# Two stacked two-layer blocks on one core: a planner with a margin on its durations, convolution taps later in its order, and gates between the head pairs of the last core

## The chip, the core and the metric

The kernel runs on one core of one Trainium2 chip. The time is device microseconds of one execution, taken over several executions; the profile is one more execution with the hardware profiler on. The engines are PE (TensorE, matmuls), DVE (VectorE), ACT (ScalarE), POOL (GpSimd) and SP (SyncE, which issues the transfers).

## What is computed

Two blocks stand one behind the other, each of two layers, for 512 tokens of width 1024 (S = 512, D = 1024), all in float32. The second block takes the output of the first.

```python
# block 1, each of 2 layers
p = rmsnorm(x) @ w_in
c_q, c_kv = rmsnorm(p[:, :384]), rmsnorm(p[:, 384:640])     # latents of q and of k, v
y_attn = mla_attention(c_q @ w_uq, c_kv @ w_ukv, rope(p[:, 640:672]))   # 8 heads
u = a * sigmoid(gt)                                         # a, gt: rest of p, 512 wide each
u = silu(layernorm(dwconv(u, 31 taps) + b))
x = x + concat(y_attn, u) @ w_o
z = dwconv(rmsnorm(x) @ w_up, 3 taps)
x = x + (silu(zg) * zv) @ w_down
# block 2, layer 0: state space mixer; layer 1: HGRN2 mixer (8 heads, chunks of 64)
z, xbc, dt = split(x @ w_in)
y = ssd(silu(conv4(xbc)), softplus(dt))       # 4 groups of 8 heads, chunks of 128
y = group_rmsnorm(y * silu(z)) @ w_out        # the "gate" is silu(z)
x = layer_norm(alpha * x + y)
x = layer_norm(alpha * x + relu(x @ w1)**2 @ w2 + gated per-layer input (PLE))
```

## The kernel before

**Tiling.** Activations lie transposed, 128 features by 512 tokens a tile. Each float32 operand is split into a rounded part and the rest (`hi`, `lo`; a copy and a subtraction), and a product is three matmuls (`mm3`: hi hi, hi lo, lo hi). A dense unit of 128 output features from 1024 inputs is `dense`: 8 x 3 = 24 matmuls of 128x512 into one PSUM bank. Sums over features go through `tok_sum`: squares on ACT, adds of [128 x 512] tiles on DVE or POOL (the last of them inside `tok_sum`), then matmuls against a column of ones (psum 128x1) or transposes; `rstd` makes 1/root on [128 x 4] tiles (DVE, then a power on POOL), and `spread` puts that back onto 128x512 by transposes of a small tile on PE.

**The order.** Nothing is issued while the model is written down. A `Recorder` records 19079 operations in the order in which the Python code calls for them; `schedule` then plans them in a list: of all operations that are ready it takes the one with the earliest start, then with the least priority number `bias - 0.015 * tail + i`, where `i` is the number in the record and `tail` the longest way to the end. `R.bias` is added to what is recorded under it: with 100, an operation stands as if it were recorded 100 operations later. The plan reckons each operation's duration by a formula (`cost`, from sizes and engine), waits between engines by a table (`LAT`), a transfer by its bytes, and an ACT table load at 1283 ns. Operations marked `either` or `other` may go to DVE or POOL, and `copy` to ACT or DVE: the plan picks. It plans POOL's work and DVE's work with two SBUF inputs not to overlap (`shares`). `SLOTS` says how many buffers of a class there are (8 PSUM banks), and `KEEP` how many of them an operation must leave free while older recorded ones still want one: 4 banks of PSUM. The resulting order on each engine, with each choice of engine, is the program; engines run their own queue in order and wait on semaphores. All instructions are issued by one line, L597, so the profile is read by tiles and by place.

**What the change touches.** `Recorder.__init__` (L330) and `cost` (L341); `KEEP` (L616); `conv_tile` (L976) in the first block's mixer, which is called behind each of the 4 head pairs of the attention: 17 taps as `SCALAR_TENSOR_TENSOR psum<-u,V,psum` on DVE into a PSUM bank and 14 taps as ACT products with POOL or DVE adds, the side; behind it come `project("w_o")` for the attention half, the convolution's layer norm (`center`, `tok_sum`, `spread`), silu, and the convolution half of `w_o`. In the state space mixer `core(g, ...)` (L1211) does one group: transposes and state products, then 4 head pairs, each with two broadcast matmuls (psum<-s,n), decays on DVE and ACT, and 64x128 products. `gate(g, ys)` (L1280) does 4 dense units with `Silu` and a product, then the group norm. The loop at the end (L1297 to L1303) records inputs and cores group by group, the last core alone (`ys[3] = core(3, *held)`), and then the 4 gates with the output projections between them. SP's queue holds the weight loads (3 buffers of class `r`).

Of the kernel before, what the change touches and what calls it, by code (L numbers as in the profile page):

```python
# [17 lines left out]
P = 128  # L18
# [301 lines left out]
class Recorder:  # L320
# [9 lines left out]
    def __init__(self):  # L330
        self.ops, self.bias, self.label, self.switch = [], 0, "", 150
        self.greed, self.order_w, self.second, self.eager, self.drag = 0.015, 1.0, 0, 0, 0.5

    def tile(self, cls, shape, dt=F32):
# [6 lines left out]

    def cost(self, eng, meth, args, kw):
        out = kw.get("out", args[0] if args else None)
        n = out.n if isinstance(out, Ap) else 1
# [270 lines left out]
SLOTS = {"psum": 8, "r": 3, "s": 86, "u": 4, "t": 12, "n": 24, "V": 1, "C": 1}  # L615
KEEP = {"psum": 4, "s": 18, "u": 2, "t": 6, "n": 16}  # L616
SIDE_TAPS = 14
# [6 lines left out]
def record(R, xT, pos, wts, vecs, consts, pT, outT, dbg=None, stop=None):  # L624
# [6 lines left out]
    def bank():  # L631
        return R.tile("psum", (P, S), F32)
# [248 lines left out]
    def mixer1(l):  # L881
# [94 lines left out]
        def conv_tile(j):  # L976
            R.label = f"conv{l}"
            acc = bank()
# [7 lines left out]
            for k in range(CONV_K - SIDE_TAPS, CONV_K):  # L986
# [4 lines left out]
                else:  # L991
                    R.either.tensor_add(side, side, t)
            R.vector.tensor_add(conv[j], acc, side)

        att = [pair() for _ in range(4)]
# [132 lines left out]
    def ssd(op):  # L1128
# [81 lines left out]

        def core(g, B, Cm, xs):  # L1211
            R.label = "ssd_core"
# [36 lines left out]
            ys = []  # L1249
            for hp in range(4):  # L1250
                py, pz = bank(), bank()
                ec = tl((P, 3 * P))
# [25 lines left out]
            return ys  # L1278

        def gate(g, ys):  # L1280
            R.label = "ssd_gate"
            for j in range(4):
                ps = bank()
                dense(ps, weights("ssd_w_in_2"), 0, P, op)
                t = tl()
                R.scalar.activation(t, ps, AF.Silu)
                R.other.tensor_mul(ys[j], ys[j], t)
            r = spread(rstd(sumsq(ys), 512, EPS2))
            out = []
            for j in range(4):  # L1290
                R.vector.scalar_tensor_tensor(ys[j], ys[j], vec("nw", g * 4 + j), r, op0=ALU.mult, op1=ALU.mult)
                hi, lo = pair()
                split_from(ys[j], hi, lo, R.either)
                out.append((hi, lo))
            return out

        ys, yo = {}, {}  # L1297
        for g in range(GROUPS):
# [3 lines left out]
            held = t  # L1302
        ys[3] = core(3, *held)  # L1303
        for g in range(GROUPS):
# [351 lines left out]
```

## Time and profile before

| | us |
|---|---|
| median of 3 executions | 2747.29 (2746.51 to 2747.91) |
| profiled execution | 2746.72 |
| its span | 2744.9 |
| PE busy in the span | 2680.1 |
| DVE, ACT, POOL busy | 1878.6, 1176.4, 775.2 |

The span runs from the first to the last instruction; 1.8 us of the profiled execution lie around it. PE is busy for 98% of the span, so what the order of the program can give back is the rest, and the stretches in which PE's clock is granted at half. The views used below give busy time of each engine by stretch of the span, with the mean granted clock (1.00 is full), and the single instructions of PE and DVE around the waits, with the idle time before each and the tile for which it waited.

The stages lie in the span as follows (us): first mixer 28 to 219 (attention from about 100), its feed forward to 680, second mixer 680 to 802, its feed forward to 1195, time steps of the state space mixer 1200 to 1222, its inputs and cores to 1430 (the last core, g = 3, from 1376), gates and output to 1600, layer norm to 1640, MLP to 1960, layer norm 1960 to 1990, HGRN2 mixer to 2270, layer norm to 2350, MLP to 2680, last layer norm and output to the end.

### The profile page before, as it was taken

Reading aid. Unit: us, or ns where it says so; the run is one execution under the profiler, and the core shown is the slowest. Engines: PE = TensorE matmul, PEld = TensorE weight load, DVE = VectorE, ACT = ScalarE, POOL = GpSimd, SP = SyncE. Lnnn points to the kernel's source line nnn. Section 1 sums busy time; section 2 is a strip of 40 time slices with the busy share of each in tenths; the row PEclk is TensorE's granted clock in tenths of the full one; section 3 lists DMA queues with packets and bytes.
Section 4 is the critical chain, followed back from the end, with each engine's and each line's share of the span. In section 5 each row is a group of like instructions: output and inputs, shape, how many; then the busy total and the mean of one; then the engine's idle time right before and its main releaser. Section 6 shows DMA issues by size and latency. Waiting matters only on the chain.

```text
span 2744.9 us, 38876 instructions
## 1 busy us (share of the span) xinstructions
PE 2680.1 (98%) x15054; PEld 2213.4 (81%) x15054; DVE 1878.6 (68%) x3319; ACT 1176.4 (43%) x2151; POOL 775.2 (28%) x645
## 2 busy tenths in 40 slices
PE   9899999999899999999989999999999999999998
PEld 7668888888678888888768898888888889888888
DVE  8997676666977766675885675445677887554546
ACT  4874323345764332343653432222356664322223
POOL 1771010134840111242331421222412123112232
PEclk9999999999999999999999999999999999999999
DMA  5031233231131223331112413223131113232320
GB/s 171 18 108 69 76 103 107 99 111 30 56 108 54 93 92 108 99 103 47 40 62 73 163 55 103 91 101 109 62 108 48 60 66 114 88 108 83 115 93 32
DMA packets 69448, 234.98 MB, mean 86 GB/s; under 512 B 7824, under 2 KB 11152, under 8 KB 69264
## 3 DMA queue, kind: packets, MB, share of 16 engines
q1 hardware_dynamic: 69264, 232.51, 25.3%
q8 instruction: 118, 1.93, 0.3%
q14 instruction: 66, 0.54, 0.1%
HBM read 230.38 MB, written 2.10 MB: 85 GB/s over the span
## 4 chain that ended last, share of the span: by engine, by line
PE 80%; DVE 15%; issue 3%; ACT 2%; POOL 0%; DMA 0%; POOLq 0%; DVEq 0%; ACTq 0%; SPq 0%
PE psum L597 80%; DVE s L597 10%; DVE psum L597 3%; ACT s L597 1%; DVE n L597 1%; ACT L597 0%; DMA r<-wts 0%; POOL n L597 0%; POOL s L597 0%; DVE u L597 0%; DVE t L597 0%; POOL u L597 0%; ACT t L597 0%; POOLq L597 0%; DVEq L597 0%
## 5 line engine op out<-in xcount | busy, mean ns | idle before, releaser
L597 PE MATMUL psum<-s,s 128*128 128x512 f32 (+3 forms) x12944 | 2604.2, 365 | 35.8 <-DVE s L597 16.0
L597 PEld LDWEIGHTS psum<-s,s 128*128 128x128 f32 (+1 forms) x12944 | 2117.8, 185 | 472.8 <-issue 27.3
L597 POOL TENSOR_TENSOR s<-r,s 128x512 fp32r<-128x512 f32 (+1 forms) x342 | 469.4, 1389 | 1062.2 <-ACT s L597 798.7
L597 ACT CAST s<-r 128x512 fp32r<-128x512 f32 (+1 forms) x721 | 407.9, 611 | 402.3 <-DMA r<-wts 390.4
L597 DVE TENSOR_TENSOR s<-s,s 128x256 f32<-128x256 f32 (+5 forms) x625 | 405.8, 672 | 76.7 <-ACT s L597 66.1
L597 DVE TENSOR_TENSOR s<-s,psum 128x512 f32<-128x512 f32 (+2 forms) x400 | 224.0, 591 | 297.6 <-PE psum L597 297.2
L597 POOL TENSOR_TENSOR s<-s,s 128x512 f32<-128x512 f32 (+4 forms) x215 | 257.1, 1206 | 514.2 <-DVE s L597 348.3
L597 DVE TENSOR_TENSOR s<-r,s 128x512 fp32r<-128x512 f32 (+1 forms) x527 | 378.2, 746 | 5.9 <-ACT s L597 3.4
L597 ACT ACTIVATE s<-s 128x512 f32<-128x512 f32 (+1 forms) x338 | 186.5, 579 | 211.8 <-DVE s L597 210.6
L597 ACT ACTIVATE s<-u,V 128x512 f32<-128x512 f32 x200 | 142.5, 763 | 264.8 <-DVE u L597 264.6
L597 ACT ACTIVATE s<-psum 128x512 f32<-128x512 f32 (+2 forms) x174 | 91.7, 528 | 373.6 <-PE psum L597 370.3
L597 DVE SCALAR_TENSOR_TENSOR s<-u,V,s 128x512 f32<-128x512 f32 x176 | 143.1, 814 | 50.0 <-ACT s L597 46.8
L597 DVE SCALAR_TENSOR_TENSOR s<-psum,s 128x512 f32<-128x512 f32 (+1 forms) x88 | 55.3, 639 | 113.4 <-ACT s L597 109.4
L597 DVE TENSOR_TENSOR u<-psum,s 128x512 f32<-128x512 f32 x88 | 60.6, 689 | 83.0 <-PE psum L597 82.8
L597 POOL TENSOR_TENSOR n<-n,n 128x4 f32<-128x4 f32 (+1 forms) x32 | 35.0, 1095 | 282.1 <-DVE n L597 281.6
L597 ACT COPY s<-psum 128x512 f32<-128x512 f32 (+4 forms) x137 | 69.6, 531 | 86.2 <-PE psum L597 85.2
L597 ACT CAST s<-s 128x512 fp32r<-128x512 f32 (+2 forms) x125 | 72.7, 592 | 75.4 <-DVE s L597 74.7
L597 DVE CAST s<-r 128x512 fp32r<-128x512 f32 (+1 forms) x148 | 62.7, 434 | 54.5 <-DMA r<-wts 54.3
L597 ACT ACT_TABLE_LOAD x68 | 87.2, 1283 | 21.2 <-DVE s L597 19.3
L597 PE MATMUL psum<-C,s 128*128 128x128 f32 (+1 forms) x532 | 80.3, 271 | 12.7 <-ACT s L597 6.0
L597 DVE SCALAR_TENSOR_TENSOR psum<-u,V,psum 128x512 f32<-128x512 f32 x128 | 91.3, 743 | 0.3
L597 PEld LDWEIGHTS psum<-C,s 128*128 128x128 f32 x532 | 63.6, 146 | 30.7 <-ACT s L597 12.8
(87 smaller groups left out, 875.3 us busy)
## 6 DMA issues: line engine op xcount, KB each, us to landing
r<-wts SPq DMA_DIRECT2D x415, 512.0 KB, 3.6
r<-wts SPq DMA_DIRECT2D x12, 256.0 KB, 2.8
r<-wts SPq DMA_DIRECT2D x8, 384.0 KB, 3.1
s<-xT SPq DMA_DIRECT2D x8, 256.0 KB, 6.1
s<-pT SPq DMA_DIRECT2D x8, 256.0 KB, 4.0
outT<-s SPq DMA_DIRECT2D x16, 128.0 KB, 1.8
r<-wts SPq DMA_DIRECT2D x9, 128.0 KB, 2.0
V<-vecs SPq DMA_DIRECT2D x1, 480.5 KB, 6.6
```

Of the source, the lines that this page charges most:

```text
L597: getattr(eng, meth)(*[res(a) for a in args], **{k: res(v) for k, v in kw.items()})
```

## The change

Four edits, and the new function `gate_unit`:

1. `self.margin = 1.12`: the plan reckons every operation but transfers as 12% longer. The waits between engines, the transfers and the table load keep their numbers.
2. `KEEP["psum"]` from 4 to 2.
3. `conv_tile` is recorded with `R.bias = 100`, so its taps, side and sum stand later in the order.
4. The dense unit of a gate becomes `gate_unit`. The 4 units of group 0 are recorded in front of the 4 head pairs of the last core; `gate(0)` then does the rest.

```diff
+        self.margin = 1.12
     def cost(self, eng, meth, args, kw):
+        return self.duration(eng, meth, args, kw) * (1.0 if eng == "sync" else self.margin)
+
+    @staticmethod
+    def duration(eng, meth, args, kw):
...
-KEEP = {"psum": 4, "s": 18, "u": 2, "t": 6, "n": 16}
+KEEP = {"psum": 2, "s": 18, "u": 2, "t": 6, "n": 16}
...
         def conv_tile(j):
-            R.label = f"conv{l}"
+            R.label, R.bias = f"conv{l}", 100
...
             R.vector.tensor_add(conv[j], acc, side)
+            R.bias = 0
...
-        def core(g, B, Cm, xs):
+        def core(g, B, Cm, xs, between=None):
...
             for hp in range(4):
+                if between:
+                    between(hp)
+                    R.label = "ssd_core"
                 py, pz = bank(), bank()
...
+        def gate_unit(ys, j):
+            R.label = "ssd_gate"
+            ps = bank()
+            dense(ps, weights("ssd_w_in_2"), 0, P, op)
+            t = tl()
+            R.scalar.activation(t, ps, AF.Silu)
+            R.other.tensor_mul(ys[j], ys[j], t)
+
         def gate(g, ys):
             R.label = "ssd_gate"
-            for j in range(4):
-                ps = bank()
-                dense(ps, weights("ssd_w_in_2"), 0, P, op)
-                t = tl()
-                R.scalar.activation(t, ps, AF.Silu)
-                R.other.tensor_mul(ys[j], ys[j], t)
+            for j in range(0 if g else 4, 4):
+                gate_unit(ys, j)
...
-        ys[3] = core(3, *held)
+        ys[3] = core(3, *held, lambda j: gate_unit(ys[0], j))
```

The record holds the same 19079 operations and the same matmuls. The order and the choices of engine come out anew over the whole program: DVE has 3006 instructions where it had 3110, POOL 694 for 637, ACT 2101 for 2048 (a few table loads among them), and SP the same 482. In the HGRN2 cores 16 operations go from DVE to POOL; in the two MLPs 35 do. Three places follow; a name is class, slot and number of a tile, `V` the vectors, `C` the constants, and the number of a tile is not the same in the two kernels. All instructions of the changed kernel are issued at L603.

**Place 1: the norms of the q and the kv latents in the first mixer (93 to 96 us).** DVE before: three `n5` rows are the norm of q, `psum2` and `psum4` rows are taps of the convolution, and `s81_885` is the last add for the sum of kv, for which PE waits.

```order
L597 TENSOR_SCALAR n5_905<-psum7_887 128x4
L597 SCALAR_TENSOR_TENSOR s66_908<-psum6_749,V0_65,s76_890 128x512
L597 TENSOR_TENSOR n5_905<-n5_905,n3_525 128x4
L597 SCALAR_TENSOR_TENSOR psum2_620<-u2_71,V0_65,psum2_620 128x512
L597 SCALAR_TENSOR_TENSOR psum4_691<-u0_67,V0_65,psum4_691 128x512
L597 TENSOR_SCALAR n5_905<-n5_905 128x4
L597 TENSOR_TENSOR s81_885<-s81_885,s85_922 128x512
L597 SCALAR_TENSOR_TENSOR s58_942<-psum0_793,V0_65,s67_927 128x512
```

DVE in the changed kernel, the same three rows of q's norm (here `n5_881`):

```order
L603 TENSOR_SCALAR n5_881<-psum7_856 128x4
L603 TENSOR_SCALAR s79_418<-s79_418,V0_65 128x512
L603 TENSOR_TENSOR n5_881<-n5_881,n3_687 128x4
L603 TENSOR_TENSOR s83_891<-r0_553,s70_804 128x512
L603 TENSOR_SCALAR n5_881<-n5_881 128x4
L603 SCALAR_TENSOR_TENSOR s77_901<-s46_786,V0_65,s79_418 128x512
L603 SCALAR_TENSOR_TENSOR s85_912<-psum0_765,V0_65,s74_899 128x512
L603 SCALAR_TENSOR_TENSOR psum1_602<-u2_71,V0_65,psum1_602 128x512
```

The add for kv (`s76_858`) stands on POOL there, behind the power of q's norm (`n6_910`):

```order
L603 TENSOR_TENSOR s57_651<-s57_651,s2_657 128x512
L603 TENSOR_TENSOR s44_583<-s44_583,s56_664 128x512
L603 TENSOR_TENSOR n6_910<-n5_881,n0_74 128x4
L603 TENSOR_TENSOR s76_858<-s76_858,s52_894 128x512
L603 TENSOR_TENSOR s57_651<-s57_651,s59_670 128x512
L603 TENSOR_TENSOR s44_583<-s44_583,s61_676 128x512
```

The last of q's three rows stood at place 152 of DVE's list and stands at 136; the taps between the three rows are gone, and the add for kv has left DVE.

**Place 2: the last core of the state space mixer (1402.7 to 1412 us).** PE before: `s35_9122,n3_2103` rows are broadcasts of a head pair, 128x128 and 64x128 rows its products.

```order
L597 MATMUL psum3_12360<-s35_9122,n3_2103 128x512
L597 MATMUL psum2_12364<-s24_12354,s29_12284 128x512
L597 MATMUL psum0_12348<-s51_11983,s18_12337 128x128
L597 MATMUL psum6_12357<-s51_11983,s18_12337 128x128
L597 MATMUL psum4_12376<-s35_9122,n3_2103 128x512
L597 MATMUL psum7_12389<-s51_11983,s83_12326 128x128
L597 MATMUL psum7_12389<-s51_11983,s18_12337 128x128
L597 MATMUL psum5_12398<-s35_9122,n3_2103 128x512
L597 MATMUL psum1_12403<-s35_9122,n3_2103 128x512
L597 MATMUL psum0_12348<-s51_11983,s17_12370 128x128
L597 MATMUL psum6_12357<-s51_11983,s17_12370 128x128
L597 MATMUL psum3_12415<-s74_12386,s38_12291 64x128
```

PE in the changed kernel around the same broadcasts (`s79_10132,n6_2355`); `psum7_12345`, `psum6_12296` and `psum3_12413` are dense units of group 0's gate:

```order
L603 MATMUL psum2_12385<-s79_10132,n6_2355 128x512
L603 MATMUL psum7_12345<-s66_10533,s50_11973 128x512
L603 MATMUL psum6_12296<-s83_10530,s15_11987 128x512
L603 MATMUL psum7_12345<-s1_10507,s37_11995 128x512
L603 MATMUL psum6_12296<-s25_10555,s60_11971 128x512
L603 MATMUL psum0_12395<-s79_10132,n6_2355 128x512
L603 MATMUL psum7_12345<-s42_10514,s26_11992 128x512
L603 MATMUL psum6_12296<-s23_10570,s60_11971 128x512
L603 MATMUL psum7_12345<-s47_10543,s26_11992 128x512
L603 MATMUL psum6_12296<-s25_10555,s15_11987 128x512
L603 MATMUL psum7_12345<-s42_10514,s38_12016 128x512
L603 MATMUL psum3_12413<-s67_10477,s56_11997 128x512
```

From the last input row to the last row of the core stood 100 core and 42 gate rows, the gate rows behind the first 98 of the core; now 100 core and 111 gate rows, and gate rows stand between core rows from the 65th core row on.

**Place 3: the layer norm behind the first MLP (1968.9 us).** PE before: the `C0_156,n16` row spreads mean and deviation, 128x512 rows with `s14_16850` belong to PLE's projection, and 128x256 rows with `s25_16658` (and `s23_16748`) need the normalized tiles.

```order
L597 MATMUL psum4_17162<-s69_16739,s14_16850 128x512
L597 MATMUL psum7_17165<-C0_156,n16_17152 128x128 x2
L597 MATMUL psum5_17168<-s69_16739,s14_16850 128x512
L597 MATMUL psum6_17173<-s69_16739,s14_16850 128x512
L597 MATMUL psum3_17186<-s80_17177,s25_16658 128x256
L597 MATMUL psum3_17186<-s81_17205,s25_16658 128x256
```

PE in the changed kernel from the spread on; the 128x256 rows that need the normalized tiles have `s67_16658`:

```order
L603 MATMUL psum6_17175<-C0_152,n16_17166 128x128 x2
L603 MATMUL psum5_17160<-s72_16754,s54_16854 128x512
L603 MATMUL psum7_17162<-s27_17157,s25_16842 128x512
L603 MATMUL psum7_17162<-s42_16750,s31_16868 128x512
L603 MATMUL psum7_17162<-s72_16754,s54_16854 128x512
L603 MATMUL psum2_17164<-s27_17157,s25_16842 128x512
L603 MATMUL psum2_17164<-s42_16750,s31_16868 128x512
L603 MATMUL psum2_17164<-s72_16754,s54_16854 128x512
L603 MATMUL psum0_17196<-s29_17185,s67_16658 128x256
L603 MATMUL psum3_17169<-s27_17157,s25_16842 128x512
L603 MATMUL psum3_17169<-s42_16750,s31_16868 128x512
L603 MATMUL psum3_17169<-s72_16754,s54_16854 128x512
```

Behind the spread stood two 128x512 rows and then a row that needs the norm; now seven stand there, then one such row, and three more 128x512 rows before the second (which stands two rows behind the last one shown). The layer norm at the end of the second MLP has the same pattern in both kernels.

## Rows read from the trace of the kernel before

**Rows 1.** Page: busy us (share) x instructions; chain of waits by engine

```profile
PE 2680.1 (98%) x15054; PEld 2213.4 (81%) x15054; DVE 1878.6 (68%) x3319; ACT 1176.4 (43%) x2151; POOL 775.2 (28%) x645
...
PE 80%; DVE 15%; issue 3%; ACT 2%; POOL 0%; DMA 0%; POOLq 0%; DVEq 0%; ACTq 0%; SPq 0%
```

**Rows 2.** Busy in a stretch of the second MLP, 128x512 matmuls alone

```profile
2400.00:2500.00 100.00, 100.00 (x436) 81.61 (x435) 50.33 (x72) 24.90 (x45) 19.73 (x16) 1.00 0.30 100
```

**Rows 3.** Waits of PE: tile <- tile waited for, total us, times, longest

```profile
PE psum L597 <- DVE s L597: 24.9, 30, 3.3
PE psum L597 <- ACT s L597: 15.6, 23, 1.7
PE psum L597 <- issue: 6.5, 3, 2.5
```

**Rows 4.** Busy by stretch: length, PE, weight loads, DVE, ACT, POOL, clock, DMA

```profile
28.00:110.00 82.00, 75.86 (x332) 60.87 (x331) 79.47 (x138) 56.45 (x94) 41.78 (x30) 0.96 0.19 60
110.00:200.00 90.00, 82.33 (x465) 57.83 (x464) 88.98 (x134) 69.03 (x150) 63.15 (x55) 1.00 0.23 77
...
680.00:790.00 110.00, 99.31 (x553) 73.42 (x552) 103.50 (x162) 84.11 (x176) 79.94 (x67) 1.00 0.22 69
...
1200.00:1222.00 22.00, 17.95 (x142) 16.51 (x141) 17.51 (x40) 10.58 (x26) 14.97 (x14) 1.00 0.18 55
...
1376.00:1430.00 54.00, 46.92 (x306) 34.29 (x305) 50.34 (x121) 31.20 (x52) 25.01 (x21) 0.97 0.08 29
...
1960.00:1990.00 30.00, 26.89 (x192) 25.51 (x192) 26.49 (x73) 15.33 (x38) 14.86 (x17) 0.89 0.11 36
...
2055.00:2270.00 215.00, 206.95 (x2770) 176.96 (x2770) 167.83 (x415) 149.23 (x288) 39.49 (x34) 0.99 0.18 60
2270.00:2350.00 80.00, 76.08 (x597) 73.30 (x596) 62.05 (x136) 31.11 (x73) 28.01 (x27) 1.00 0.28 94
...
2680.00:2700.00 20.00, 16.85 (x119) 15.62 (x118) 19.29 (x53) 8.19 (x19) 9.08 (x11) 0.91 0.01 2
```

**Rows 5.** Timeline of PE, 47 to 102: start, us, operation, [idle before <- releaser]

```profile
50.55 1.11 PE L597 MATMUL psum<-C,n 128*128 128x128 f32 x4 [2.53 <-POOL n L597]
...
96.52 1.05 PE L597 MATMUL psum<-C,s 128*128 128x1 f32 x8 [3.35 <-DVE s L597]
```

**Rows 6.** Timeline of PE, 692 to 700 us, the second mixer

```profile
696.99 1.09 PE L597 MATMUL psum<-C,n 128*128 128x128 f32 x8 [3.32 <-DVE n L597]
```

**Rows 7.** Timeline of PE, 1967.5 to 1979 us, behind the spread

```profile
1970.50 0.38 PE L597 MATMUL psum<-s,s 128*128 128x256 f32 x1 [0.70 <-ACT s L597]
1973.18 1.01 PE L597 MATMUL psum<-s,s 128*128 128x256 f32 x3 [2.30 <-DVE s L597]
```

**Rows 8.** Timeline of PE, 2684 to 2692 us, the last layer norm

```profile
2687.72 0.62 PE L597 MATMUL psum<-s,s 128*128 128x256 f32 x3 [2.30 <-DVE s L597]
```

**Rows 9.** Timeline of PE, 112 to 130 us, the attention

```profile
121.02 0.50 PE L597 MATMUL psum<-s,s 128*128 128x512 f32 x1 [1.03 <-DVE s L597]
```

**Rows 10.** Timeline of PE, 1395 to 1430 us, the last core

```profile
1405.36 0.50 PE L597 MATMUL psum<-s,n 128*128 128x512 f32 x1 [0.64 <-DVE s L597]
...
1411.32 5.41 PE L597 MATMUL psum<-s,s 128*128 128x128 f32 x44 [1.06 <-DVE s L597]
```

**Rows 11.** Page, groups: operation xcount | busy us, mean ns | idle before

```profile
L597 POOL TENSOR_TENSOR s<-s,s 128x512 f32<-128x512 f32 (+4 forms) x215 | 257.1, 1206 | 514.2 <-DVE s L597 348.3
L597 DVE TENSOR_TENSOR s<-r,s 128x512 fp32r<-128x512 f32 (+1 forms) x527 | 378.2, 746 | 5.9 <-ACT s L597 3.4
...
L597 DVE SCALAR_TENSOR_TENSOR psum<-u,V,psum 128x512 f32<-128x512 f32 x128 | 91.3, 743 | 0.3
```

**Rows 12.** Timeline of PE, 195 to 222 us, centre of the convolution's norm

```profile
199.60 1.12 PE L597 MATMUL psum<-s,t 128*128 128x512 f32 x2
```

**Rows 13.** Timeline of DVE, 197 to 222 us, its first split

```profile
215.11 0.42 DVE L597 CAST s<-s 128x512 fp32r<-128x512 f32 x1
```

**Rows 14.** Timeline of DVE, 100 to 118 us, beside POOL

```profile
108.05 1.72 DVE L597 TENSOR_TENSOR s<-r,s 128x512 fp32r<-128x512 f32 x1
```

## The prediction

> **What bounds the kernel now.** The page comes first. PE is busy 98% of the span and has 80% of the chain of waits, DVE 15% [rows 1]. So the kernel is bound by PE's work, which this change leaves as it is. What an order can win is the span less PE's busy time, 2744.9 - 2680.1 = 64.8 us, and what a lower clock costs. In a dense stretch 436 matmuls of 128x512 took 100.00 us, PE busy for all of it [rows 2]: 0.229 us each, the price of a PE row that covers a wait. PE's waits are put down mostly to DVE's tiles (24.9 us in 30 waits) and ACT's (15.6 us in 23) [rows 3].
>
> Next, the table by stretch, for where that time lies [rows 4]. The reader is to see that idle stands in few stretches, and a lower granted clock beside it. For each I add the idle time and (1 - clock) x length, which is what is lost while the clock stands at 1.2 in place of 2.4 GHz:
>
> - 28 to 110: 82.00 - 75.86 = 6.1 idle, 0.04 x 82 = 3.3 clock: 9.4
> - 110 to 200: 7.7, clock full
> - 680 to 790: 10.7, clock full
> - 1200 to 1222: 4.1, clock full
> - 1376 to 1430: 7.1 + 0.03 x 54 = 8.7
> - 1960 to 1990: 3.1 + 0.11 x 30 = 6.4
> - 2055 to 2270: 8.1 + 0.01 x 215 = 10.2
> - 2270 to 2350: 3.9, clock full
> - 2680 to 2700: 3.2 + 0.09 x 20 = 5.0
>
> Together 66 us, the most that this change can work on. In the first three stretches and the last core DVE is busy for 79.47 of 82, 88.98 of 90, 103.50 of 110 and 50.34 of 54 us: there DVE is the bound, and what matters is how much of its work stands ahead of each row for which PE waits. Behind the layer norms it is how many PE rows cover DVE's chain.
>
> Last, the waits themselves. The longest are 2.53 us at 50.55 (the first norm) and 3.35 at 96.52 (the sum of kv) [rows 5], 3.32 at 696.99 [rows 6], 0.70 and 2.30 behind the spread at 1970 [rows 7], and 2.30 at 2687.72 [rows 8]. Shorter ones stand in the attention, as 1.03 at 121.02 [rows 9], and in the last core [rows 10].
>
> **The change part by part.** Operations and matmuls are the same, so no edit has a cost of its own; each moves rows. The margin does it everywhere, by making operations look long against the waits and transfers that keep their numbers; the bias and the gates do it in two places.
>
> *28 to 110.* In front of DVE's first norm row stand 8 rows fewer (place 72 for 80), and PE has 12 rows to do before the spread for 10. The norm came 2.53 us late [rows 5]; I leave 0.7 of it: 1.8 won. The add for kv stood behind the last row of q's norm, at place 152 of DVE; that row now has place 136. Sixteen rows at 0.58 us (DVE's mean here, 79.47 / 138 [rows 4]) are 9 us, so PE's sum for q sets the time then, and not DVE's queue. The add itself is on POOL, behind the power of q's norm, and takes 1.2 us there [rows 11]; PE has 10 rows more (2.3 us) to do before it needs the result. The wait of 3.35 closes but for 0.3: 3.0 won. Each of these waits was followed by half clock; of those 3.3 us I take 2.3. Sum 7.
>
> *110 to 200.* The bias lets the taps be passed. The splits of the first head pair's Q and K stood at places 182 to 190 of DVE and stand at 154 to 168; the last attention row has place 296 for 310, the last tap 287 for 284. DVE's rows up to the convolution's norm become fewer by some 14, or 8 to 10 us. DVE is 98% busy from 28 to 200, so both stretches can win what DVE loses, about 10, and the 3 us that DVE is idle: 13 at most. I take 4 here, 11 for both. What is late next is the chain of the convolution's norm: from the centre's matmul at 199.60 [rows 12] to the first split at 215.53 [rows 13] it took 15.9 us. From that matmul to the first row of `w_o`'s convolution half PE had 99 rows (22.7 us) and has 74 (places 765 to 839): 16.9 us. That covers it by 1 us, and I cost it at nothing, with -1 as a bound; without that cover it is the slower rival below.
>
> *680 to 790.* The same in the second layer. The wait of 3.32 [rows 6] shrinks by 2.8, since the norm's rows come earlier; the splits stand at place 805 for 830, the last attention row at 938 for 963, the last tap at 929 for 902. DVE's 6.5 us of idle leave more room, and the convolution's cover stays 94 rows. I take 7 of 10.7.
>
> *1200 to 1222.* The norm's spread stands 3 PE rows later, and three `lo` tiles stand one behind another on POOL. Bounds 0 and -1.6; I take -1.
>
> *1376 to 1430.* The first 64 rows of the core, to about 1390, have no gate row between them, as before, so they keep their waits. Behind them four waits, from 0.64 at 1405.36 to 1.06 at 1411.32 [rows 10], are 2.8 us, and the clock's fall 1.6; 0.6 more stands in front of them. Up to the last core row stand 111 gate rows for 42: 69 x 0.229 = 16 us of cover for these 5.0. The rows come from a stretch behind that stays dense. With them 4 `Silu`, 4 products and some table loads come into the core's queues; POOL (25.01 of 54 us busy) and ACT (31.20) have room [rows 4]. I take 4.
>
> *1960 to 1990 and 2680 to 2700.* Behind the spread stood two 128x512 rows and then a row of the norm; now 7 and 3 more, eight more in all, 1.8 us of cover for 0.70 and 2.30 [rows 7], and DVE has two products fewer in front of the second tile (0.4 us each). The rows taken from ahead of the spread covered nothing that waited. I leave 1 us of idle; the half clock behind it (3.3, and 1.8) then mostly goes: 5 and 3.5 won.
>
> *2055 to 2270.* Sixteen operations of the HGRN2 cores go to POOL. DVE and ACT have 167.83 and 149.23 us of work in 215 [rows 4], so there is slack; the three `issue` waits (6.5 us [rows 3]) are not waits for another engine's tile, and stay. Bounds -6 and 3; I take 0. *2270 to 2350:* 16 more MLP rows stand before the first row that waited: 2 won of 3.9. The dense stages stay.
>
> *New waits.* A list planned anew waits where none did. The nearest rows are PE's waits for ACT, 15.6 us in 23 [rows 3], 0.7 each: I take 4 of them, -3, with 0 and -12 as bounds.
>
> Sum: 7 + 4 + 7 - 1 + 4 + 5 + 3.5 + 0 + 2 - 3 = 28.5. From the profiled execution, 2746.7, that is 2718.2; the median stands 0.6 above it. I say 2718. With half of what is won (32.5 / 2 = 16) and new waits at their bound, 4 us are left: 2743. With all that the terms name (13 + 10.7 + 5 + 6.4 + 5 + 3.9 = 44) and 3 in the HGRN2 mixer: 2700.
>
> **The rivals.** *The load comes back through POOL.* DVE has 104 rows fewer, POOL 57 more. A DVE subtraction beside POOL took 1.72 us at 108.05 [rows 14], where its group's mean is 0.746 [rows 11]: 1 us more. As a mechanism here: eight more POOL rows in the first two mixers each cost DVE 1 us where it is the bound, 8 lost, and DVE no longer runs ahead, so that the mixers win half, 9 less: 2718 + 17 = 2735. Against it, taps read one tile from SBUF, and the plan keeps POOL and such DVE work apart. The Trainium skill, "SBUF — State Buffer", section "SBUF: two separate sides", states that a DVE instruction with two SBUF inputs and a POOL one that reads SBUF lock each other out for a whole instruction; the row at 108.05 agrees with that.
>
> *The plan does not do what it says.* The plan of before foresaw no such waits either. If a longer reckoning only shifts them to other tiles, the mixers win nothing, and the layer norms (8.5) and the core (4) stand against new waits at their bound, 12: no change, 2747. For it speaks that 53 waits on DVE and ACT [rows 3] are spread over a whole program that is planned anew.
>
> *Slower: the taps come too late.* The norm of the convolution cannot start before the last tap. Between the last attention row and the centre's matmul PE has 11 rows (2.5 us), and the cover behind it 1 us: 3.5 us, or 5 taps of 0.743 us [rows 11], can end behind the attention at no cost; each further tap costs its 0.743 us in each layer. It outweighs the 28.5 us when each layer loses 14.3, from (14.3 + 3.5) / 0.743 = 24 taps; at 40 of the 68 it is 2 x (29.7 - 3.5) = 52 lost: 2770. Against it, the attention's last row stands behind the last tap on DVE in both layers.
>
> **How the numbers follow.** The forecast has 0.62, with its own range from 2700 to 2743; the load on POOL 0.15 (2735); waits only shifted 0.12 (2747, to either side); taps too late 0.08 (2770); 0.03 for more than the listed gains. The range from 2698 to 2744 leaves out the slower rival, most of the third case and the tail below, 2 in 10. A measurement tells about 0.2%, 5.5 us, from no change: faster is below 2741.8. Faster: 0.61 + 0.15 + 0.03 = 0.79; within 0.2%: 0.10 of the shifted waits and 0.01 of the forecast, 0.11; slower: 0.08 + 0.02 = 0.10.
>
> **What would show it.** In the table by stretch of the changed kernel: idle of 2 us in place of 6.1 between 28 and 110 with the clock above 0.98; DVE still over 95% busy in the attention, with about 4 us of idle in each mixer; no wait above 0.5 us in the core's second half; the clock at 0.97 or more behind the two spreads; dense stages still full. It would be wrong if the mixers' idle stayed near 18 us with DVE's subtractions well above 0.75 us (POOL), if waits of over 1 us stood where PE had none (shifted), or if PE waited for the convolution's centre behind the attention (slower).

## The result

The changed kernel takes 2716.45 us (median of 4 executions, 2715.73 to 2719.6); the kernel before took 2746.9 beside it. The ratio is 0.9893, 95% interval 0.9876 to 0.9910: 29 us less by the ratio, 1.1%, where 2718 us had been forecast. Over all runs and chips the kernel before took 2743.84 to 2754.78 us, so what follows compares ratios, each to the kernel before on the same chip.

The page of the changed kernel, with busy time, share and count of each engine and the chain of waits by engine [rows 1]:

```profile
PE 2666.4 (98%) x15054; PEld 2214.5 (82%) x15054; DVE 1859.3 (69%) x3215; ACT 1214.9 (45%) x2206; POOL 831.4 (31%) x702
...
PE 94%; DVE 4%; ACT 1%; issue 1%; DMA 0%; POOL 0%; SPq 0%; ACTq 0%; POOLq 0%; DVEq 0%
```

DVE's part of the chain fell from 15% to 4%. PE's idle is 2714.0 - 2666.4 = 47.6 us, for 64.8; PE's busy time fell by 13.7 us with the same matmuls. Half clock hides in it: 18 matmuls of 128x512 took 4.29 us at 98.36 and 5.84 at 107.46, behind a long wait, and the granted clock from 107 to 110 was 0.54 (both are shown below). PE's waits (tile, tile waited for, total, times, longest) are as many us on DVE as before and half as many on ACT [rows 3]:

```profile
PE psum L603 <- DVE s L603: 24.4, 21, 4.8
PE psum L603 <- ACT s L603: 7.8, 11, 1.6
PE psum L603 <- issue: 7.6, 5, 3.3
```

A longest wait on DVE of 4.8 us is new. Since all stages shift in time, I matched every PE instruction of the two traces to its recorded operation and compared when the last one of a stage ends. The shares, in us won in the profiled executions (spans 2744.9 and 2714.0), beside what was forecast:

| stage | forecast | won |
|---|---|---|
| start, first mixer to the last row of its inputs | 7 | 10.0 |
| first attention, `w_o`, feed forward | 4 | -1.9 |
| second mixer and feed forward | 7 | 13.2 |
| time steps, inputs of the state space mixer | -1 | 1.9 |
| last core and gates | 4 | 6.9 |
| output, layer norm, first MLP | 0 | -1.3 |
| layer norm behind the first MLP | 5 | 0.5 |
| HGRN2 mixer | 0 | 2.8 |
| its layer norm, second MLP | 2 | -0.2 |
| last layer norm and end | 3.5 | -1.0 |
| new waits, anywhere | -3 | (in the rows above) |
| sum | 28.5 | 30.9 |

The sum came out 2.4 us from the forecast, and several of its rows miss by 3 to 6 us, to both sides: that they cancel is luck. The stretches in which PE waited before, in the changed kernel (length, PE, weight loads, DVE, ACT, POOL, clock, DMA share [rows 4]):

```profile
28.00:107.00 79.00, 74.66 (x343) 61.10 (x341) 73.94 (x125) 57.42 (x94) 37.50 (x29) 1.00 0.19 59
107.00:110.00 3.00, 2.54 (x6) 2.11 (x7) 2.64 (x5) 0.00 (x0) 0.03 (x1) 0.54 0.00 0
110.00:200.00 90.00, 84.30 (x475) 61.52 (x475) 85.22 (x130) 63.19 (x139) 61.13 (x56) 0.98 0.13 43
680.00:771.00 91.00, 89.54 (x512) 66.24 (x511) 87.10 (x138) 72.75 (x155) 64.04 (x57) 1.00 0.14 43
1353.00:1374.00 21.00, 16.01 (x120) 11.55 (x118) 20.00 (x50) 16.53 (x28) 12.35 (x11) 0.99 0.07 25
1374.00:1417.00 43.00, 43.00 (x253) 34.11 (x254) 33.15 (x70) 25.99 (x39) 13.95 (x13) 0.96 0.12 38
```

The second mixer is nearly full now (1.5 us idle in 91). The core's second half, from 1374, is full, and its first half keeps its waits. Between 28 and 107 the waits for the first norm and for the sum of kv are gone and the clock is full; all 4.3 us of idle there are one new wait, which ends at 107.46. PE, then DVE, then POOL around it (start, length, operation, idle before):

```profile
98.36 4.29 PE L603 MATMUL psum<-s,s 128*128 128x512 f32 x18
107.46 5.84 PE L603 MATMUL psum<-s,s 128*128 128x512 f32 x18 [4.81 <-DVE s L603]
```

```profile
101.30 1.40 DVE L603 SCALAR_TENSOR_TENSOR psum<-u,V,psum 128x512 f32<-128x512 f32 x2
102.61 5.04 DVE L603 CAST s<-s 128x512 fp32r<-128x512 f32 x2
107.57 2.12 DVE L603 TENSOR_TENSOR s<-s,s 128x512 fp32r<-128x512 f32 x3
```

```profile
95.83 11.20 POOL L603 TENSOR_TENSOR s<-s,s 128x512 fp32r<-128x512 f32 x9 [0.99 <-DVE s L603]
114.96 0.13 POOL L603 MEMSET u<- 128x1 f32 x2 [7.93 <-DVE psum L603]
```

Two casts that take 0.42 us each took 5.04 together (the first 4.71 of them), and came free when POOL's nine adds and subtractions, 1.25 us each and without a pause, ended at 107.03. PE waits for the first cast, the `hi` part of the first head pair's Q.

The plan had foreseen this clash. The section on the order names only DVE's work with two SBUF inputs, but `shares` keeps copies from SBUF to SBUF apart from POOL's work as well. In the plan's own times POOL pauses from 103.1 to 105.9 us, and DVE's two casts and the subtractions behind them fall into that pause. In the program there is only the order of each queue: POOL had nothing to wait for and went on.

### The profile page after: what moved, and what is told of

It reads as the page before. It is cut to its first block, busy times and chain, and to the rows that moved or that the text cites. A ratio compares the mean times of both kernels' runs of the same rounds, so it can differ in the third digit from the quotient of the medians.

```text
span 2714.0 us, 38873 instructions
## 1 busy us (share of the span) xinstructions
PE 2666.4 (98%) x15054; PEld 2214.5 (82%) x15054; DVE 1859.3 (69%) x3215; ACT 1214.9 (45%) x2206; POOL 831.4 (31%) x702
## 4 chain that ended last, share of the span: by engine, by line
PE 94%; DVE 4%; ACT 1%; issue 1%; DMA 0%; POOL 0%; SPq 0%; ACTq 0%; POOLq 0%; DVEq 0%
PE psum L603 94%; DVE s L603 3%; ACT s L603 1%; DVE psum L603 0%; POOL s L603 0%; DVE n L603 0%; DMA s<-xT 0%; DMA r<-wts 0%; ACT L603 0%; SPq L603 0%; POOL n L603 0%; ACTq L603 0%; POOLq L603 0%; DVEq L603 0%
## 5 line engine op out<-in xcount | busy, mean ns | idle before, releaser
L603 PE MATMUL psum<-s,s 128*128 128x512 f32 (+5 forms) x12944 | 2601.0, 365 | 34.7 <-DVE s L603 22.8
L603 PEld LDWEIGHTS psum<-s,s 128*128 128x128 f32 (+2 forms) x12944 | 2118.8, 185 | 459.0 <-issue 35.3
L603 POOL TENSOR_TENSOR s<-r,s 128x512 fp32r<-128x512 f32 (+1 forms) x371 | 509.2, 1386 | 1122.6 <-ACT s L603 869.3
L603 ACT CAST s<-r 128x512 fp32r<-128x512 f32 (+1 forms) x738 | 420.4, 613 | 380.0 <-DMA r<-wts 369.2
L603 DVE TENSOR_TENSOR s<-s,s 128x512 fp32r<-128x512 f32 (+4 forms) x605 | 398.8, 681 | 75.0 <-ACT s L603 66.1
L603 DVE TENSOR_TENSOR s<-s,psum 128x512 f32<-128x512 f32 (+2 forms) x400 | 225.5, 592 | 280.7 <-PE psum L603 278.6
L603 POOL TENSOR_TENSOR s<-s,s 128x512 f32<-128x512 f32 (+5 forms) x235 | 265.7, 1143 | 444.6 <-ACT s L603 249.3
L603 DVE TENSOR_TENSOR s<-r,s 128x512 fp32r<-128x512 f32 (+1 forms) x498 | 359.5, 749 | 8.5 <-ACT s L603 6.3
L603 ACT ACTIVATE s<-s 128x512 f32<-128x512 f32 (+1 forms) x338 | 187.1, 577 | 195.0 <-DVE s L603 193.7
L603 ACT ACTIVATE s<-u,V 128x512 f32<-128x512 f32 x200 | 143.4, 761 | 257.8 <-DVE u L603 257.6
L603 ACT ACTIVATE s<-psum 128x512 f32<-128x512 f32 (+2 forms) x174 | 91.5, 527 | 349.7 <-PE psum L603 347.7
L603 DVE SCALAR_TENSOR_TENSOR s<-u,V,s 128x512 f32<-128x512 f32 x176 | 145.5, 827 | 49.0 <-ACT s L603 47.1
L603 DVE SCALAR_TENSOR_TENSOR s<-psum,s 128x512 f32<-128x512 f32 (+1 forms) x88 | 55.5, 639 | 106.9 <-ACT s L603 106.5
L603 ACT CAST s<-s 128x512 fp32r<-128x512 f32 (+2 forms) x139 | 81.7, 594 | 99.5 <-DVE s L603 94.3
L603 DVE TENSOR_TENSOR u<-psum,s 128x512 f32<-128x512 f32 x88 | 60.7, 690 | 85.1 <-PE psum L603 84.8
L603 ACT COPY s<-psum 128x512 f32<-128x512 f32 (+4 forms) x149 | 75.7, 537 | 88.4 <-PE psum L603 87.3
L603 POOL TENSOR_TENSOR n<-n,n 128x4 f32<-128x4 f32 (+1 forms) x32 | 36.2, 1131 | 185.2 <-DVE n L603 184.9
L603 DVE SCALAR_TENSOR_TENSOR psum<-u,V,psum 128x512 f32<-128x512 f32 x128 | 92.4, 745 | 0.1
L603 PE MATMUL psum<-C,s 128*128 128x128 f32 (+1 forms) x532 | 85.3, 272 | 4.5 <-ACT s L603 4.1
L603 DVE CAST s<-r 128x512 fp32r<-128x512 f32 (+1 forms) x131 | 59.4, 466 | 41.1 <-DMA r<-wts 40.9
L603 DVE SCALAR_TENSOR_TENSOR s<-psum,V,s 128x511 f32<-128x511 f32 (+4 forms) x90 | 65.6, 744 | 26.2 <-ACT s L603 21.5
```

The source lines that it names most:

```text
L603: getattr(eng, meth)(*[res(a) for a in args], **{k: res(v) for k, v in kw.items()})
```

## The experiments

The section on the change says that the plan reckons every operation but transfers 12% longer. That is wrong. In the code, matmuls are reckoned by `cost_tensor`, which does not go through `cost`: the margin reaches DVE, ACT and POOL, and PE keeps its numbers.

### Each edit taken back

```diff
-        self.margin = 1.12
+        self.margin = 1.0
```

> The changed kernel with margin 1.0: bias, PSUM and gates stay. Theory: the margin carries the larger part of the gain outside the core, since it is the only edit that reaches the norms of the first mixer and all later stages; some 15 us of the 30 go, 2732 us, with the last core still about 7 us shorter than before the change. Rival (a list that is planned anew comes out a few us better or worse at each stage by chance, whatever the edit): stages move by several us to both sides and the time is anywhere from 2715 to 2750.

2746.71 us, ratio 0.9985 (0.9975 to 0.9994): without the margin almost the whole gain goes, more than forecast. The first mixer's front wins 0.9 us in place of 10.0, the second mixer and feed forward 2.0 in place of 13.2; the core keeps 5.5 of 6.9.

```diff
-KEEP = {"psum": 2, "s": 18, "u": 2, "t": 6, "n": 16}
+KEEP = {"psum": 4, "s": 18, "u": 2, "t": 6, "n": 16}
```

> The changed kernel with 4 PSUM banks kept for older operations. Theory: no stage of before waited for a PSUM bank, so this edit has no share of its own: 2717 us, within 3. Rival (chance of the list): 2715 to 2750, with single stages 3 us or more to either side.

0.9897 (0.9882 to 0.9912), the changed kernel's ratio within the interval, as the theory had it. Its profiled execution loses 5.6 us in the second mixer and feed forward against the changed kernel, so single stages do move.

```diff
-            R.label, R.bias = f"conv{l}", 100
+            R.label = f"conv{l}"
```

> The changed kernel with the convolution recorded without bias. Theory: the two mixers give back about half of the 20 us that they won (28 to 219 and 680 to 802 of before), the rest stays: 2727 us. Rival (the margin alone makes the mixers shorter, the bias is of no account): 2717 us, mixers unchanged within 2 us.

0.9919 (0.9904 to 0.9933), 7 us above the changed kernel, where some 10 had been forecast. The place is not quite as told: the first attention with `w_o` and feed forward loses 12 us against the changed kernel, more than the medians differ by (the profiled execution is the slowest of this kernel's), and the second mixer 2. A cast is in it again; DVE, POOL and PE:

```profile
153.16 6.37 DVE L603 CAST s<-s 128x512 fp32r<-128x512 f32 x1
```

```profile
150.58 8.65 POOL L603 TENSOR_TENSOR s<-s,s 64x512 fp32r<-64x512 f32 x7 [2.32 <-ACT s L603]
```

```profile
159.67 4.61 PE L603 MATMUL psum<-s,s 128*128 128x512 f32 x16 [4.74 <-DVE s L603]
```

The cast ends behind the seventh of POOL's operations without a pause, and PE's wait is 4.74 us. So a part of the 7 us may be this cast and not the place of the taps; the run does not part them.

```diff
-        ys[3] = core(3, *held, lambda j: gate_unit(ys[0], j))
+        ys[3] = core(3, *held)
```

(and `gate` with all four units again)

> The changed kernel with the gates of group 0 recorded behind the last core, as before. Theory: everything up to the last core is as in the changed kernel, and the core gives back its 7 us, with the waits of PE in its second half: 2723 us. Rival (the core is shorter for the margin's sake, the gates would have filled it anyway): 2717 us.

0.9899 (0.9884 to 0.9914), 2 us or less above the changed kernel: the rival's number. Everything up to the core has the same order row for row and ends within 1 us of the changed kernel, and the core wins 6.0 us without the gates between its head pairs.

### The margin alone

The kernel before with the first edit only:

```diff
+        return self.duration(eng, meth, args, kw) * (1.0 if eng == "sync" else self.margin)   # margin 1.12
```

> The kernel before with nothing but the margin of 1.12, which in the code reaches DVE, ACT and POOL operations and not PE's. Theory (the plan reckons these three engines too fast against PE, and the margin mends that): the margin alone carries most of the gain, 20 of 30 us, 2727 us; the taps' bias then adds some 7 and the gates 2. Rival (the edits only work together, or a new list wins by chance): 2740 us or more.

2731.52 us, 0.9926 (0.9911 to 0.9941): 20 us of the 29, as the theory had it. But its core wins nothing (2.3 us are lost there). With the runs above this settles the core. From the last input row to the last core row, less 0.229 us for each gate row in between:

| kernel | KEEP of PSUM | gates between | core rows ahead of the first gate row | gate rows | us without them |
|---|---|---|---|---|---|
| before | 4 | no | 98 | 42 | 43.2 |
| margin alone | 4 | no | 99 | 42 | 47.5 |
| no gates | 2 | no | 84 | 52 | 38.9 |
| 4 banks kept | 4 | yes | 71 | 111 | 38.3 |
| no margin | 2 | yes | 64 | 122 | 38.5 |
| changed kernel | 2 | yes | 64 | 111 | 38.1 |

Either edit is enough, and the second adds nothing that shows. With 4 banks kept for older operations a gate unit recorded behind the core gets no bank while the core still wants some, so no gate row can pass; 2 kept banks let it in, and so does recording it earlier.

### The size of the margin

```diff
-        self.margin = 1.12
+        self.margin = 1.06        # and 1.18, 1.11, 1.13
```

> The changed kernel with margin 1.06. Theory: it mends half of what the plan has wrong and lies between the kernel without a margin (about 3 us below before) and the changed kernel (30 below): 2730 us, 2724 to 2738. Rival (chance of the list): anywhere from 2712 to 2750, also above the one without a margin or below the changed kernel.

> The changed kernel with margin 1.18. Theory: the plan reckoned 1637 us of DVE where the profile of before has 1878.6 (15% more), so 1.18 is as near as 1.12: 2712 to 2722 us. Rival (1.12 was a lucky number of the list): 10 us or more above the changed kernel.

> The changed kernel with margin 1.11. The run with 1.18 lost all but 4 us, so the theory of a plan that is mended by a truer reckoning is in doubt. If there is a range of good margins around 1.12: 2713 to 2721 us. If 1.12 is one good list among many (the rival): 1.11 and 1.13 scatter by 5 to 25 us above the changed kernel, with the losses at other places in each, above all in the first attention and the first `w_o`.

> The changed kernel with margin 1.13; as for 1.11: 2713 to 2721 us if there is a good range, 5 to 25 us above the changed kernel if each margin is one more draw of a list.

| margin | ratio | interval |
|---|---|---|
| 1.00 | 0.9985 | 0.9975 to 0.9994 |
| 1.06 | 0.9954 | 0.9938 to 0.9971 |
| 1.11 | 0.9906 | 0.9892 to 0.9921 |
| 1.12 | 0.9893 | 0.9876 to 0.9910 |
| 1.13 | 0.9915 | 0.9899 to 0.9932 |
| 1.18 | 0.9985 | 0.9975 to 0.9994 |

1.06 lies between, as the theory wants, but in its number only: by stages the front of the first mixer wins 1.0 us of the 10.0 and the second mixer with its feed forward 1.0 of the 13.2, while the first attention to feed forward wins 8.7, where the changed kernel loses 1.9. 1.18 lies 25 us above the changed kernel, against the theory. 1.11 and 1.13 are 3.5 and 6 us above 1.12 by their ratios, at the upper edge of the one theory's band and at the foot of the other's 5 to 25; the three intervals overlap, so the times do not tell these margins apart. There is a range of good margins, then, and it ends before 1.18. Single stages move within it all the same, as the rival said: the front of the first mixer wins 6.9 us with 1.11, 10.0 with 1.12 and 10.7 with 1.13.

Two places take most of what 1.18 loses. The first is `w_o` of the first layer. PE with margin 1.18:

```profile
204.72 3.89 PE L603 MATMUL psum<-s,s 128*128 128x512 f32 x16
211.43 1.88 PE L603 MATMUL psum<-s,t 128*128 128x512 f32 x2 [2.82 <-DVE s L603]
218.84 1.87 PE L603 MATMUL psum<-C,s 128*128 128x1 f32 x8 [5.53 <-DVE s L603]
222.43 1.11 PE L603 MATMUL psum<-C,n 128*128 128x128 f32 x4 [1.73 <-POOL n L603]
226.84 1.65 PE L603 MATMUL psum<-s,s 128*128 128x512 f32 x3 [3.29 <-DVE s L603]
```

These are the centre's matmul, the sums, the spread and the first row of the convolution's half, in sequence: 13.4 us of waits for the convolution's norm, with all 96 rows of the attention half already done. It is the slower rival of the prediction. In this order 9 taps stand behind the last attention row on DVE, with six adds of finished `w_o` tiles between them (no tap does in the changed kernel, nor at 1.11 and 1.13 in either layer). The stage loses 14 us against the changed kernel.

The second is the layer norm behind the first MLP. The stage loses 11 us there against the changed kernel with 1.18, and 5 to 6 with 1.06 and with 1.11. Behind the spread PE's next matmul for a mean, that of the second half of the tokens (`psum<-s,t`), has to wait for a sum that DVE adds up behind its rows for the first half. PE at this matmul, with margins 1.12, 1.11 and 1.18:

```profile
1944.07 0.70 PE L603 MATMUL psum<-s,t 128*128 128x256 f32 x2 [0.31 <-DVE s L603]
```

```profile
1949.59 1.22 PE L603 MATMUL psum<-s,t 128*128 128x256 f32 x2 [4.23 <-DVE s L603]
```

```profile
1965.87 1.22 PE L603 MATMUL psum<-s,t 128*128 128x256 f32 x2 [4.84 <-DVE s L603]
1974.89 1.22 PE L603 MATMUL psum<-s,s 128*128 128x512 f32 x2 [7.80 <-DVE s L603]
```

The fewer rows PE has between the spread and this matmul, the longer it waits:

| kernel | rows between | wait there, us |
|---|---|---|
| margin on PE too | 15 | 0 |
| margin 1.12 (changed) | 11 | 0.31 |
| margin 1.13 | 10 | 0.78 |
| margin alone | 7 | 1.27 |
| no margin | 4 | 3.52 |
| margins 1.06 and 1.11 | 2 | 4.21, 4.23 |
| margin 1.18 | 0 | 4.84 |

In the kernel before 6 rows stand there, and four of them need the norm and have their own waits, 0.70 and 2.30 [rows 7]. The wait of 7.80 us behind the matmul, with 1.18, is for a `lo` tile of PLE's projection.

### The margin on PE's operations too

```diff
-            o.alts = [(eng, self.cost_tensor(calls), calls)]
+            o.alts = [(eng, self.margin * self.cost_tensor(calls), calls)]
```

> The changed kernel with the margin on PE's operations too, which it leaves out. Theory (it matters how the three engines are reckoned against PE): the list is near that without a margin, 2735 to 2750 us, and the front of the first mixer gets none of its 10 us. Rival (it matters how operations are reckoned against the fixed waits and transfers): 2712 to 2725, front of the mixer as in the changed kernel.

2745.78 us, 0.9989 (0.9979 to 0.9998): the gain is gone. What matters is how DVE, ACT and POOL are reckoned against PE, and not operations against waits and transfers, as the prediction had said. The front of the first mixer still wins 4.7 us of 10.0, where none was expected. Why it would be the ratio of the engines: the plan of before adds up its DVE operations to 1637 us and POOL's to 687, where the page has 1878.6 and 775.2 [rows 1], 15 and 13% more; PE's come to 2619, for 2680.1, 2% more. A plan with DVE that much too fast puts a row of PE where DVE has not got to yet.

A rival to this stands untested. With the margin the plan also gives DVE less to do: the page counts 3319 DVE instructions before, 3317 without a margin and 3313 with PE's margin too, against 3204 to 3223 with margins from 1.11 to 1.18; in the changed kernel 57 operations more are POOL's and 47 more ACT's. A lighter DVE is not enough, since 1.18 has 3208 and no gain. But no run keeps the choice of engines and changes the order alone.

### Two places of the finished order

In the changed kernel's order, POOL's four adds of the convolution's side from 102 to 107 us go to DVE behind the first scores. Behind the spreads at the ends of both MLPs, DVE's fourth and fifth tile go ahead of the centring of the second half. `put(R, ids, behind)` takes operations out of the planned order and puts them behind another one.

```diff
     R.schedule(SLOTS, KEEP)
+    put(R, [807, 973, 809, 975], 727, "vector")
+    put(R, [13010, 13014, 13011, 13015], 13003)
+    put(R, [18360, 18364, 18361, 18365], 18353)
```

> The changed kernel with two places of its finished order moved, all else kept row for row. First, the four adds of the convolution's side that POOL does from 102.1 to 107.0 us go to DVE, behind the scores of the first head pair. If DVE's cast of 4.71 us at 102.61 is held up by POOL's run of adds, it takes 0.4 us and PE's wait of 4.81 at 107.46 falls below 1; if it is held up by anything else, both stay. Second, behind the spreads of the layer norms at the end of both MLPs DVE makes the fourth and the fifth tile of the first half before it centres the second half. If PE's waits of 2.95 at 1949.43 and 2660.94 are this order of DVE, they fall to about 1; if they are the chain's length, they stay or move to the second half. In all 2 to 4 us at the first place and 1 to 2 at each of the others: 2711 us; by the rivals 2716.

2714.33 us, 0.9867 (0.9852 to 0.9882): the fastest of all, though its interval overlaps that of the changed kernel. DVE and PE at the first place:

```profile
101.92 1.40 DVE L603 SCALAR_TENSOR_TENSOR psum<-u,V,psum 128x512 f32<-128x512 f32 x2
103.23 0.75 DVE L603 CAST s<-s 128x512 fp32r<-128x512 f32 x2
```

```profile
103.79 4.39 PE L603 MATMUL psum<-s,s 128*128 128x512 f32 x18 [0.51 <-DVE s L603]
...
115.66 2.08 PE L603 MATMUL psum<-s,s 128*128 128x512 f32 x4 [3.81 <-DVE s L603]
118.62 5.68 PE L603 MATMUL psum<-s,s 128*128 128x512 f32 x17 [0.89 <-DVE s L603]
```

Both casts take 0.75 us together and PE's wait is 0.51 for 4.81. It was POOL's run that held the cast. Some of that is given back: the next waits are 3.81 and 0.89, for 1.34 and 1.77, since DVE now has the adds. Behind the spread, before (the changed kernel) and after the move:

```profile
1944.07 0.70 PE L603 MATMUL psum<-s,t 128*128 128x256 f32 x2 [0.31 <-DVE s L603]
1944.42 2.06 PE L603 MATMUL psum<-s,s 128*128 128x256 f32 x9
1949.43 0.74 PE L603 MATMUL psum<-s,s 128*128 128x256 f32 x4 [2.95 <-DVE s L603]
```

```profile
1941.85 2.05 PE L603 MATMUL psum<-s,s 128*128 128x256 f32 x9
1945.04 0.86 PE L603 MATMUL psum<-s,s 128*128 128x256 f32 x5 [1.14 <-DVE s L603]
1947.03 3.31 PE L603 MATMUL psum<-s,s 128*128 128x256 f32 x15 [1.13 <-ACT s L603]
```

2.95 became 1.14, as expected, and 1.13 on ACT came behind it: half a microsecond won. DVE's order was the first cause of that wait and the chain through ACT is the next. Behind the second MLP 2.95 became 1.15, 0.80 on ACT and 0.44. By stages the first attention with `w_o` and feed forward won 3.1 us against the changed kernel, and both norms together nothing; the 7 us between the two ratios are more than these places explain.

### The same cast in another form

```diff
-    tensor_copy(hi, src)
+    tensor_tensor(out=hi, in0=src, in1=src, op=ALU.max)
```

for the two casts alone, in the finished order of the changed kernel.

> The changed kernel in which two casts on DVE, the one of 4.71 us at 102.61 and the next, are made as a maximum of a tile with itself: the same result, read through two SBUF inputs; order and engines stay row for row. Theory (a cast from SBUF to SBUF is passed over by POOL's queued adds, while an operation with two SBUF inputs gets its turn behind the running one): the first takes at most 1.9 us and PE's wait of 4.81 falls to between 1 and 2.5. Rival (whatever DVE asks for there has to wait for the end of POOL's run): it takes 4.4 us or more and PE's wait stays.

2718.49 us, 0.9886 (0.9866 to 0.9906), no difference in time. DVE, POOL and PE:

```profile
102.97 1.28 DVE L603 TENSOR_TENSOR s<-s 128x512 fp32r<-128x512 f32 x2
104.17 4.06 DVE L603 TENSOR_TENSOR s<-s,s 128x512 fp32r<-128x512 f32 x3
```

```profile
96.18 14.43 POOL L603 TENSOR_TENSOR s<-s,s 128x512 fp32r<-128x512 f32 x9 [0.99 <-DVE s L603]
```

```profile
103.79 2.11 PE L603 MATMUL psum<-s,s 128*128 128x512 f32 x8 [0.78 <-DVE s L603]
106.60 0.73 PE L603 MATMUL psum<-s,s 128*128 128x512 f32 x2 [0.71 <-DVE s L603]
108.29 2.12 PE L603 MATMUL psum<-s,s 128*128 128x512 f32 x8 [0.95 <-DVE s L603]
```

The two take 1.28 us, and POOL's nine operations 14.43 in place of 11.20: now DVE gets its turn, and POOL waits for it. PE's first wait falls from 4.81 to 0.78 (under what was expected), with 0.71 and 0.95 behind it, as the three subtractions take 4.06 in place of 2.12.

That the form did it is not shown. The kernel without the gates between the head pairs has the casts as they were, and the same order here; DVE and POOL in its trace:

```profile
102.52 2.68 DVE L603 CAST s<-s 128x512 fp32r<-128x512 f32 x2
```

```profile
95.74 12.87 POOL L603 TENSOR_TENSOR s<-s,s 128x512 fp32r<-128x512 f32 x9 [0.99 <-DVE s L603]
```

There the unchanged cast got its turn too (1.25 us, the second 1.50), POOL was the one to wait, and PE's waits were 1.36, 0.26, 0.17 and 0.46. So in two executions of one order the cast was passed over once and once not.

## Why the prediction was right, point by point

**What bounds the kernel.** Right: PE's waits on DVE where DVE is nearly full, and the half clock behind the long ones. The idle of the second mixer fell as DVE's rows came earlier. Of the signs that the prediction named, the full dense stages and the full second half of the core came. The idle of 28 to 110 is 4.8 us and not 2, DVE is 94.7% busy in the attention and not over 95, the clock behind the two spreads is 0.94 and 0.93 and not 0.97, and one wait of over 1 us stands where PE had none.

**28 to 110.** Right in mechanism, 10.0 us for 7. Both waits [rows 5] are gone whole, where 0.7 and 0.3 had been left, and so is the half clock.

**110 to 200.** Wrong: -1.9 us for 4. The step that failed is "both stretches can win what DVE loses": it let DVE pass its saved work on, as if DVE stayed the bound. DVE did lose its work: from 28 us to its last row of the attention, its rows add up to 162 us at the times usual for their forms, 11 less than before, as reckoned. But it was idle for 10.8 us there in place of 4.0: it waited 4.2 us for ACT's tiles and 4.8 for PE's, where it had been 0.4 and 0.6. The largest new wait of PE is the one for the cast, 4.81 us. That wait is not the whole step: where the cast came free sooner, the stage lost 2.6 us (no gates) or won 0.3 (the other form) and 1.2 (POOL's adds moved), and not 4. Both stretches together gave 8.1 of 11.

**680 to 790.** Undersized, 13.2 us for 7: the wait for the norm [rows 6] is gone whole, and the attention followed.

**The last core.** 6.9 us for 4, right in place: nothing waits in its second half, and its first half keeps its waits. The cause was half right: gate rows between core rows do cover the waits, but the kept PSUM banks let them in as well, and the step "no edit has a cost of its own; each moves rows" gave `KEEP` no share to look for. Recording the gates earlier brought 2 us or less.

**The layer norms behind the MLPs.** Wrong: 0.5 and -1.0 us for 5 and 3.5. "I leave 1 us of idle" followed DVE to its first `lo` tiles only. Their rows wait no more, where 0.70 and 2.30 had been waited [rows 7]; the 0.31 us at 1944.07 are for the mean of the second half. The fourth `lo` tile is late, since eight rows stand ahead of it on DVE, five of them the centring of the second half, and 2.95 us are waited there. The half clock that was to go mostly stayed, 0.94 and 0.93 for 0.89 and 0.91 [rows 4]:

```profile
1935.00:1965.00 30.00, 26.60 (x181) 24.56 (x180) 25.02 (x68) 13.52 (x32) 10.96 (x14) 0.94 0.11 36
...
2655.00:2680.00 25.00, 21.62 (x156) 20.42 (x155) 22.00 (x60) 12.08 (x29) 9.30 (x11) 0.93 0.07 22
```

**HGRN2, time steps, new waits.** HGRN2 won 2.8, within its bounds. The time steps with the inputs behind them won 1.9 where 1 was to be lost. New waits there are, not four of 0.7 us but one of 4.81 and the two of 2.95.

**The reason for the margin.** Wrong: not operations against fixed waits and transfers, but the other engines against PE, as far as the rival of the lighter DVE leaves it. The number did not rest on it, since its terms came from the order.

**The rivals.** The load on POOL is real at one place, the cast. It is not the 1 us for each row that moved: up to the last attention row the DVE rows that were held took 16.9 us longer than is usual for their forms, and 16.2 before. Late taps are one of the two places where margin 1.18 loses, with 9 taps, near the 5 from which the prediction let them cost something. Their price was set too low: 13.4 us of waits stand behind them and not 0.743 us for each above 5, since PE had by then done all rows that could cover the chain. The chance of the plan that only shifts its waits should have been higher: 1.18 loses nearly everything, and single stages of 1.11 and 1.13 lie some us off.

**Still open:** whether the truer order or the lighter DVE carries the margin's gain, and what the first attention lacks when the cast comes free.

## What to carry to other kernels

Where a plan sets the order, compare its sum for each engine with the profile's busy time: here two engines were reckoned 13 to 15% too fast against the bounding one, and correcting that won 0.7% alone. After such a correction try the neighbours of the number too, since each is a new order and single stages move by 5 to 15 us. A pause that the plan leaves on one engine for the sake of another is not in the program, unless something is waited for there. When a covered wait is costed, follow the chain past its first tile to the last one that the covered rows need.

## What the hardware showed that was not expected

A DVE instruction on SBUF can be passed over by a whole run of POOL's queue. In the changed kernel 214 DVE instructions took over 0.06 us longer than is usual for their form; 213 of them by at most 1.14 us, about one POOL instruction, and the cast by 4.28. In the kernel without a margin one cast took 8.85 us, next to POOL's 7.38 us of subtractions without a pause. DVE, then POOL, of that kernel:

```profile
170.34 8.85 DVE L603 CAST s<-s 128x512 fp32r<-128x512 f32 x1
```

```profile
169.04 2.51 POOL L603 TENSOR_TENSOR s<-s,s 64x512 fp32r<-64x512 f32 x2 [0.68 <-ACT s L603]
171.52 7.38 POOL L603 TENSOR_TENSOR s<-r,s 128x512 fp32r<-128x512 f32 x6
```

The Trainium skill, "SBUF — State Buffer", section "SBUF: two separate sides", has the port that the two share held for one whole instruction; these rows show a loser that waits for several. With two inputs the same cast got its turn in the last experiment, but so did the unchanged one in the kernel without the gates. Nor are two inputs safe: with the margin on PE too, a subtraction with two SBUF inputs was passed over by three POOL instructions, though not by the whole run. DVE, then POOL:

```profile
130.38 5.95 DVE L603 TENSOR_TENSOR s<-s,s 64x512 fp32r<-64x512 f32 x2
```

```profile
130.94 1.18 POOL L603 TENSOR_TENSOR s<-r,s 128x256 fp32r<-128x256 f32 x1
132.08 9.08 POOL L603 TENSOR_TENSOR s<-s,s 128x512 f32<-128x512 f32 x7
```

The two subtractions take 5.95 us, 0.7 each elsewhere; the second, from 131.56, took 4.78 and ended at 136.33, while POOL went on to 141.16. Which instruction is passed over, and when, these runs do not settle.
